# A hybrid SSD and pooling trunk on one core: input transposes and the dt projection moved ahead of the input norm, with the stored transpose as residual

## The chip, the cores and the metric

The kernel runs on one core of a Trainium2 chip. The metric is the device time of one execution in microseconds (us). Engines: PE (tensor engine, with PEld as its weight load), DVE (vector), ACT (scalar), POOL (GpSimd) and SP (which issues DMAs).

## The reference, cut to what matters

272 tokens (16 learned meta tokens and 256 of the input) of width 2048 pass two layers; every sub-layer is wrapped in norms, `h = h + post_norm(f(pre_norm(h)))`. Layer 0 is a Mamba-2 mixer and an FFN, layer 1 a pooling mixer and an FFN. All is float32.

```python
def rmsnorm(x, w):
    return x * rsqrt(mean(x * x, axis=-1) + 1e-6) * w
...
def ssd_mixer(u, w_in, ...):
    z, xBC, dt_raw = split(u @ w_in, [4096, 4096 + 6144])   # the last 64 columns are dt_raw
    xBC = silu(causal_depthwise_conv(xBC, conv_w, conv_b))
    dt = softplus(dt_raw + dt_bias)
    ...
def reference(...):
    h = concatenate([meta, x], axis=1)
    for i in range(2):
        u = rmsnorm(h, norm_w[i, 0])
        mix = ssd_mixer(u, ...) if i % 2 == 0 else pool_mixer(u, ...)
        h = h + rmsnorm(mix, norm_w[i, 1])
        f = swiglu(rmsnorm(h, norm_w[i, 2]), ...)
        h = h + rmsnorm(f, norm_w[i, 3])
    return h[:, 16:]
```

## The kernel before, in words

Activations lie transposed: channels on the 128 partitions, the 272 tokens along the row, as 16 slices of 128 channels. Every weight matrix is cut into panels (`Panel`) of 512 columns as a rule. A panel is streamed in steps: SP loads 512 KB or 1 MB of raw weights into one of three buffers (`emit_dma`, L147), ACT rounds a piece to the format that PE multiplies in one pass (`whi`, `emit_hi`, L162), DVE computes what the rounding left over (`wlo`, `emit_lo`, L175; called the weight rest below), and PE makes three products per 128x128 block: rounded weight with rounded activation, rounded weight with the activation's rest, weight rest with rounded activation (L275 to L277). The activations are kept in the same two parts, `uhi` and `ulo`, the two halves of the tile `uu`. Products of two unrounded fp32 tiles are issued too; the profile shows each of these as two records.

`run_stream` (L241) walks over all steps in a fixed order and emits the casts two steps ahead. Each engine works off its queue in the order in which instructions were emitted. Smaller work is emitted between products as generators (`gen_...`) in three lists, at places set by a rough clock in the program (`Clock`).

`startup` (L1208) loads meta tokens (`mt`) and input (`xt`) with tokens on partitions, sums squares on ACT and DVE into `ssq`, which POOL zeroes first, and makes the factors `rs`. Then, slice by slice and interleaved with the steps of the first panel B0, it scales the tokens (L1283 to L1290), transposes them on PE with three instructions a slice (L1301, L1303), and turns the result into `uhi` (ACT, L1304) and `ulo` (DVE, L1305), both read from PSUM. Panel dt (64 columns, each loaded twice so that all 128 partitions of the result are filled) follows B0 with the usual three products, then come C0 and the panels of x and z. SP issues the eleven small parameter loads (L1233) after the input and the first weights.

For the residual, `gen_h` (L754) loads x and the meta tokens again during panel oB, the output projection's second half, and transposes 8 of the 16 slices between products of oB; the other 8 are transposed in `junction` (L883), at the start of the first FFN, after the row of the norm is finished. The other junctions have seven unused products there (`warm`, L643) that keep PE at work while DVE takes the reciprocal. After it `Producer` makes the normed slices: the sum h, `uu` rounded by ACT (L717), its rest by DVE (L727).

Of the kernel before, what the change touches and what calls it, by code (L numbers as in the profile page):

```python
# [15 lines left out]
P = 128  # L16
# [51 lines left out]
def trunk_kernel(ctx: ExitStack, tc: tile.TileContext, x, meta, norm_w, w_in, conv_w, conv_b,  # L68
# [230 lines left out]
    cs_dram = dram.tile([64, T], F32, name="cs_dram")  # L299
    S = {"conv": 0}  # L300
# [23 lines left out]
    def evac_dt(m, a):  # L324
        S["dtw"] = [S["pool"].tile([P, CBW], F32, name="M", bufs=5) for i in range(5)]
        nc.scalar.activation(out=S["dtw"][0][:, :T], in_=a[:, :T], func=AF.Identity, bias=dtb)

    def gen_dt():
        dtcs = S["dtcs"]
        v, e, z, z2, q = [t[:, :T] for t in S["dtw"]]  # L330
# [3 lines left out]
        t = ck.act(T * 3, f="exp")  # L334
# [418 lines left out]

    def gen_h():  # L754
        f = F["pool"]
        h = F["h"]
        for c in range(4):
            cs_ = slice(c * 512, (c + 1) * 512)
            xr = f.tile([P, 2, 512], F32, name="xr", bufs=2)
            mr = f.tile([NM, 512], F32, name="mr", bufs=2)  # L760
            nc.sync.dma_start(out=xr, in_=x_f[:, cs_].rearrange("(i p) c -> p i c", p=P))
            nc.sync.dma_start(out=mr, in_=meta[:, cs_])
            t = ck.t["PE"] + 4.0
            if c >= 2:
                F["late_h"].append((c, xr, mr))
                yield "PE", t
                continue
            for k in range(4):
                ks_ = slice(k * P, (k + 1) * P)
                yield "py", t  # L770
                tp = bank("py")
                locks.add("py")
                nc.tensor.transpose(tp[:, 0:NM], mr[:, ks_], ident[0:NM, 0:NM])
                for i in range(2):
                    nc.tensor.transpose(tp[:, NM + i * P:NM + (i + 1) * P], xr[:, i, ks_], ident)
                t = ck.pe(0.25)
                yield "ACT", t
                nc.scalar.copy(out=h[:, c * 4 + k, :], in_=tp[:, :T])
                locks.discard("py")
                t = ck.act(T)  # L780
# [137 lines left out]
    p_dt()  # L918
# [289 lines left out]
    def startup(st):  # L1208
        start = st.enter_context(tc.tile_pool(name="start", bufs=1, reuse_waits="tile"))
        xt = start.tile([P, 2, D], F32, name="xt")  # L1210
        mt = start.tile([NM, D], F32, name="mt")
        prow = start.tile([P, 4, P], F32, name="prow")
        nc.scalar.preload_act_table(AF.Sqrt)
        nc.sync.dma_start(out=mt, in_=meta)
        for c in range(2):
            cs_ = slice(c * 1024, (c + 1) * 1024)
            for i in range(2):
                nc.sync.dma_start(out=xt[:, i, cs_], in_=x_f[i * P:(i + 1) * P, cs_])
        nc.sync.dma_start(out=prow[:, 0, :], in_=norm_w.rearrange("a b (k p) -> (a b k) p", p=P))
        emit_dma(2)  # L1220
        cw = conv_w[0].rearrange("a (k p) -> (a k) p", p=P)
        dbc = start.tile([P, 64], F32, name="dbc")
        for dst, src in ((prow[:, 1, :], cw[0:128, :]), (prow[0:64, 2, :], cw[128:192, :]),
# [9 lines left out]
            nc.sync.dma_start(out=dst, in_=src)  # L1233
# [17 lines left out]
        sqd = start.tile([P, 1024], F32, name="sqd")

        def sq_act(i, q, c0, c1):
            n, src = (NM, mt[:, c0:c1]) if i == 2 else (P, xt[:, i, c0:c1])
            nc.scalar.activation(out=sqj[0:n, c0:c1], in_=src, func=AF.Square, accum_out=ssq[0:n, i, q:q + 1])

        def sq_dve(i, q, c0, c1):
            nc.vector.scalar_tensor_tensor(out=sqd[:, 0:c1 - c0], in0=xt[:, i, c0:c1], scalar=1.0,
                                           in1=xt[:, i, c0:c1], op0=ALU.mult, op1=ALU.mult,
                                           accum_out=ssq[:, i, q:q + 1])  # L1260

        sq_act(2, 0, 0, 1024)
        sq_act(2, 1, 1024, 2048)
        sq_act(0, 0, 0, 1024)
        sq_dve(1, 0, 0, 1024)
        sq_act(0, 1, 1024, 2048)
        sq_dve(1, 1, 1024, 1536)
        sq_act(1, 2, 1536, 2048)
        tp = bank("pt")
        nc.tensor.transpose(tp[:, 0:P], prow[:, 0, :], ident)  # L1270
        nc.vector.tensor_copy(out=pv[:, 0:P], in_=tp[:, 0:P])
        nc.vector.tensor_reduce(out=rs, in_=ssq, op=ALU.add, axis=mybir.AxisListType.X)
        nc.scalar.activation(out=rs, in_=rs, func=AF.Sqrt, scale=1.0 / D, bias=eps)
        nc.vector.reciprocal(out=rs, in_=rs)

        ends = (256, 512, 1024, 1536, 2048)
        scaled = [0]

        def scale(k):
            while scaled[0] <= k * P:  # L1280
                c0 = scaled[0]
                c1 = scaled[0] = next(e for e in ends if e > c0)
                nc.scalar.activation(out=mt[:, c0:c1], in_=mt[:, c0:c1], func=AF.Copy, scale=rs[0:NM, 2:3])  # L1283
                nc.vector.tensor_scalar(out=xt[:, 0, c0:c1], in0=xt[:, 0, c0:c1], scalar1=rs[:, 0:1], scalar2=None,
                                        op0=ALU.mult)
                if c0 == 0:
# [64 lines left out]
```

## Time and profile before

| | |
|---|---|
| median of 3 runs | 2398.69 us (2398.11 to 2400.9) |
| profiled execution: own time, span | 2399.69 us, 2397.6 us |
| busy: PE, DVE, ACT, POOL | 99%, 60%, 49%, 1% |
| chain that ended last | PE 96%, DVE 2%, ACT 1% |
| mean granted PE clock | 0.998 of full speed |
| DMA | 418 MB, 174 GB/s |

A row of the timeline gives start, duration, engine, source line, operation, the written tile, the read tiles and the shape; in brackets how long the engine sat idle before and what it waited for. Matmuls are pipelined, so the distance between two starts, and not the duration, is what one costs PE.

### The profile page before, as it was taken

How to read it: one execution, taken by the hardware profiler on the slowest of the kernel's cores; microseconds unless marked ns; L12 is line 12 of the kernel's file. 1: busy time of each engine (PE TensorE's matmuls, PEld its weight loads, DVE VectorE, ACT ScalarE, POOL GpSimd, SP SyncE). 2: the span in 40 equal slices, each digit the busy share in tenths (PEclk: the TensorE clock that was granted, in tenths of full speed). 3: DMA queues.
4: the chain of work that ended last, by engine and by line, in shares of the span. 5: the costliest groups of instructions: out<-in, count | busy, mean ns of one | idle time of the engine just before them, and what ended most of it. 6: DMA issues, size and time to landing. Idle time of an engine off the chain costs nothing.

```text
span 2397.6 us, 39491 instructions
## 1 busy us (share of the span) xinstructions
PE 2364.3 (99%) x16660; PEld 2219.0 (93%) x16660; DVE 1447.8 (60%) x1927; ACT 1180.2 (49%) x1605; POOL 13.8 (1%) x38
## 2 busy tenths in 40 slices
PE   7999999999999999999999999999999999999998
PEld 7999999999999999999999999988888888888886
DVE  5878867647865855454445454578666554556655
ACT  6656565445654644443344443456544444444443
POOL 0000000000000000000000000010000000000000
PEclk9999999999999999999999999999999999999999
DMA  6555555555554555565555555433665655565554
GB/s 190 170 165 182 177 167 176 170 176 178 176 178 158 147 189 175 163 189 176 176 176 173 179 176 176 167 120 106 191 195 173 192 195 192 177 199 187 197 189 141
DMA packets 203825, 418.37 MB, mean 174 GB/s; under 512 B 9920, under 2 KB 10416, under 8 KB 203504
## 3 DMA queue, kind: packets, MB, share of 16 engines
q1 hardware_dynamic: 203216, 415.07, 53.9%
q8 instruction: 130, 2.13, 0.4%
q10 hardware_dynamic: 432, 0.79, 0.1%
q14 instruction: 47, 0.39, 0.0%
HBM read 413.66 MB, written 2.17 MB: 173 GB/s over the span
## 4 chain that ended last, share of the span: by engine, by line
PE 96%; DVE 2%; ACT 1%; issue 0%; DMA 0%; SPq 0%; DVEq 0%; ACTq 0%
PE acc_g L271 7%; PE acc_u L271 7%; PE acc_g L276 4%; PE acc_g L277 4%; PE acc_d L277 4%; PE acc_g L275 4%; PE acc_u L275 4%; PE acc_u L277 4%; PE acc_u L276 4%; PE acc_d L276 4%; PE acc_d L275 4%; PE acc_g L273 3%; PE acc_u L273 3%; PE acc_z L275 3%; PE acc_z L277 3%; PE acc_z L276 3%
## 5 line engine op out<-in xcount | busy, mean ns | idle before, releaser
L175 DVE TENSOR_TENSOR wlo<-raw,whi 128x1024 fp32r<-128x1024 f32 (+2 forms) x804 | 936.9, 1167 | 772.3 <-ACT whi L162 767.7
L162 ACT CAST whi<-raw 128x1024 fp32r<-128x1024 f32 (+2 forms) x800 | 803.1, 1005 | 951.6 <-PE acc_u L276 149.3
L271 PE MATMUL acc_g<-uu,whi 128*128 128x512 f32 x704 | 248.5, 396 | 2.5 <-DVE uu L727 1.3
L271 PE MATMUL acc_u<-uu,whi 128*128 128x512 f32 x704 | 247.0, 394 | 0.2 <-DVE g L789 0.2
L275 PE MATMUL acc_g<-uu,whi 128*128 128x272 f32 x704 | 204.8, 291 | 0.9 <-ACT uu L717 0.9
L277 PE MATMUL acc_g<-uu,wlo 128*128 128x272 f32 x704 | 203.8, 289 | 0.0
L276 PE MATMUL acc_g<-uu,whi 128*128 128x272 f32 x704 | 203.5, 289 | 0.1
L277 PE MATMUL acc_u<-uu,wlo 128*128 128x272 f32 x704 | 203.2, 289 | 0.0
L277 PE MATMUL acc_d<-hidhi,wlo 128*128 128x272 f32 x704 | 203.2, 289 | 0.0
L275 PE MATMUL acc_u<-uu,whi 128*128 128x272 f32 x704 | 203.1, 288 | 0.0
L276 PE MATMUL acc_u<-uu,whi 128*128 128x272 f32 x704 | 202.7, 288 | 0.0
L275 PE MATMUL acc_d<-hidhi,whi 128*128 128x272 f32 x704 | 202.3, 287 | 0.0
L276 PE MATMUL acc_d<-hidlo,whi 128*128 128x272 f32 x704 | 202.2, 287 | 0.0
L273 PE MATMUL acc_g<-uu,wlo 128*128 128x256 f32 x704 | 197.2, 280 | 0.7 <-DVE wlo L175 0.7
L273 PE MATMUL acc_u<-uu,wlo 128*128 128x256 f32 x704 | 197.0, 280 | 0.0
L271 PEld LDWEIGHTS acc_g<-uu,whi 128*128 128x128 f32 x704 | 132.1, 188 | 34.9 <-DVE ups L815 1.9
L271 PEld LDWEIGHTS acc_u<-uu,whi 128*128 128x128 f32 x704 | 132.1, 188 | 32.0 <-DVE g L789 0.6
L275 PE MATMUL acc_z<-uu,whi 128*128 128x272 f32 x512 | 150.7, 294 | 0.0
L275 PE MATMUL acc_x<-uu,whi 128*128 128x272 f32 x512 | 150.2, 293 | 0.0
L277 PE MATMUL acc_x<-uu,wlo 128*128 128x272 f32 x512 | 147.6, 288 | 0.0
L277 PE MATMUL acc_z<-uu,wlo 128*128 128x272 f32 x512 | 147.6, 288 | 0.0
L276 PE MATMUL acc_x<-uu,whi 128*128 128x272 f32 x512 | 147.4, 288 | 0.0
(384 smaller groups left out, 5250.0 us busy)
## 6 DMA issues: line engine op xcount, KB each, us to landing
raw<-in_ffn_w_down_dram SPq DMA_DIRECT2D x88, 1024.0 KB, 5.0
raw<-in_ssd_w_in_dram SPq DMA_DIRECT2D x76, 1024.0 KB, 5.3
raw<-in_ffn_w_gate_dram SPq DMA_DIRECT2D x64, 1024.0 KB, 5.2
raw<-in_ffn_w_up_dram SPq DMA_DIRECT2D x64, 1024.0 KB, 5.2
raw<-in_ssd_w_out_dram SPq DMA_DIRECT2D x32, 1024.0 KB, 5.1
raw<-in_ffn_w_gate_dram SPq DMA_DIRECT2D x32, 768.0 KB, 4.5
raw<-in_ffn_w_up_dram SPq DMA_DIRECT2D x32, 768.0 KB, 4.5
bc<-cs_dram SPq DMA_DIRECT2D x32, 272.0 KB, 6.0
```

Source lines behind the costliest of these rows:

```text
L162: nc.scalar.copy(out=s["hi"], in_=raw)
L175: nc.vector.tensor_tensor(out=s["lo"][:, :, sl], in0=raw, in1=s["hi"].bitcast(F32)[:, :, sl], op=ALU.subtract)
L271: nc.tensor.matmul(a[:, :2 * p.n].rearrange("p (a c) -> p a c", c=p.n), lhsT=wh, rhs=p.both(k), start=st, stop=False)
L273: nc.tensor.matmul(a[:, p.n:2 * p.n], lhsT=wl, rhs=xh, start=False, stop=en)
L275: nc.tensor.matmul(a[:, :p.n], lhsT=wh, rhs=xh, start=st, stop=False)
L276: nc.tensor.matmul(a[:, :p.n], lhsT=wh, rhs=xl, start=False, stop=False)
L277: nc.tensor.matmul(a[:, :p.n], lhsT=wl, rhs=xh, start=False, stop=en)
```

## The change

1. The residual: the transposed raw tokens are kept. They lie in `part`, are written to a DRAM tensor `xT_dram` by four DMAs from POOL, and are read back into `h` by four DMAs from POOL when the FFN's pool opens. `gen_h` and the transposes in `junction` are gone; the first junction gets the seven warming products of the others.
2. The start: all 16 slices of raw tokens are transposed first. ACT copies each into `part`. The dt projection is made from these raw slices with plain fp32 products, two of 64 columns a slice into the two halves of the accumulator, interleaved with the transposes; its weights `wdt` are multiplied by the norm's weights on DVE, and its result by the token factors `rb` in `gen_dt`. The row `rb` is spread over partitions by PE at slice 10.
3. The normed slices are made from `part`: DVE multiplies by weight and `rb`, ACT rounds, DVE subtracts. Five are emitted beside the transposes, the others ahead of B0's steps. B0 is streamed in steps of two slices instead of one.
4. Loads: the norm weights come first, x comes in eight pieces of both token tiles, the meta tokens on ACT's queue, the dt weights between the x pieces, three B0 loads instead of two. The eleven parameter loads are issued by POOL, ahead of its zeroing of `ssq`.

```diff
+    xT_dram = dram.tile([P, KD, T], F32, name="xT_dram")
...
-    def gen_dt():
+    def gen_dt(a):
...
+        nc.vector.tensor_tensor(out=v, in0=a[:, :T], in1=rb, op=ALU.mult)
+        t = ck.dve(T + 60)
+        yield "ACT", t
+        nc.scalar.activation(out=v, in_=v, func=AF.Identity, bias=dtb)
...
-        add_panel(Panel(nm, wi[:, c0:c0 + 512], 16, xhl, T, evac_raw, ku=2 if nm == "B0" else 4, ks=1 if nm == "B0" else 2, 
-                        after=lambda: add_work("A", nm, gen_bc(kind, half))))
+        add_panel(Panel(nm, wi[:, c0:c0 + 512], 16, xhl, T, evac_raw, after=lambda: add_work("A", nm, gen_bc(kind, half))))
...
-        F["late_h"] = []
+        for c in range(4):
+            nc.gpsimd.dma_start(out=F["h"][:, c * 4:c * 4 + 4, :], in_=xT_dram[:, c * 4:c * 4 + 4, :])
...
         def pre():
             if l1 == 0:
-                flush("h")
                 open_hidden()
             F["ss"].row(rb)
-            if l1 == 0:
-                for c, xr, mr in F["late_h"]:
...
-                        nc.scalar.copy(out=F["h"][:, c * 4 + k, :], in_=tp[:, :T])
-            else:
-                F["ss"].warm(WARM)
+            F["ss"].warm(WARM)
             recip(rb, n)
...
     p_bc("B", 0)
-    p_dt()
     p_bc("C", 0)
...
+        nc.scalar.dma_start(out=mt, in_=meta)
+        for c in range(8):
+            cs_ = slice(c * 256, (c + 1) * 256)
+            nc.sync.dma_start(out=xt[:, :, cs_], in_=x_f[:, cs_].rearrange("(i p) c -> p i c", p=P))
+            if c % 4 == 0:
+                k8 = slice(c * 2, c * 2 + 8)
+                nc.sync.dma_start(out=wdt[:, k8, :], in_=wi[c * 256:c * 256 + 1024, 10240:10304].rearrange(
+                    "(k p) c -> p k c", p=P))
+        emit_dma(3)
...
-            nc.sync.dma_start(out=dst, in_=src)
+            nc.gpsimd.dma_start(out=dst, in_=src)
...
         nc.gpsimd.memset(ssq, 0.0)
...
+        def factor_row():
+            tp = bank("py")
+            for n, c0 in parts:
+                nc.tensor.matmul(tp[:, c0:c0 + n], lhsT=ones[0:n, 0:P], rhs=dg[0:n, c0:c0 + n], start=True, stop=True)
+            nc.scalar.copy(out=rb, in_=tp[:, :T])
...
+        def turn(k):
+            ks_ = slice(k * P, (k + 1) * P)
+            tp = acc_tile() if k % 2 else bank("pt")
+            nc.tensor.transpose(tp[:, 0:NM], mt[:, ks_], ident[0:NM, 0:NM])
+            for i in range(2):
+                nc.tensor.transpose(tp[:, NM + i * P:NM + (i + 1) * P], xt[:, i, ks_], ident)
+            nc.scalar.copy(out=part[:, k, :], in_=tp[:, :T])
+
+        def dt_mm(k):
+            for d in range(2):
+                nc.tensor.matmul(acc_dt[64 * d:64 * d + 64, :T], lhsT=wdt[:, k, :], rhs=part[:, k, :],
+                                 start=k == 0, stop=k == KD - 1)
...
+                v = start.tile([P, T], F32, name="v", bufs=3)
+                nc.vector.scalar_tensor_tensor(out=v, in0=part[:, k, :], scalar=nw(0, 0, k), in1=rb, op0=ALU.mult,
+                                               op1=ALU.mult)
+                nc.scalar.copy(out=uhi[:, k, :], in_=v)
+                nc.vector.tensor_tensor(out=ulo[:, k, :], in0=v, in1=uhi[:, k, :].bitcast(F32), op=ALU.subtract)
...
+        nc.scalar.activation(out=sqm[0:NM], in_=mt, func=AF.Square, accum_out=ssq[0:NM, 2, 0:1])
+        dummies(5)
...
+        for k in range(KD):
+            turn(k)
+            if k == 0:
+                dummies(2, P)
...
+                    nc.vector.tensor_tensor(out=wdt[:, k8, :], in0=wdt[:, k8, :], in1=nwk[:, k8, :], op=ALU.mult)
+                    squares(2 * h)
+                    squares(2 * h + 1)
+                factors()
+            else:
+                dt_mm(k - 1)
+            if k == 10:
+                factor_row()
+            if k >= 11:
+                upto(k - 10)
+            if k == 12:
+                emit_hi(1)
+                emit_lo(1)
+        dt_mm(KD - 1)
+        for c in range(4):
+            nc.gpsimd.dma_start(out=xT_dram[:, c * 4:c * 4 + 4, :], in_=part[:, c * 4:c * 4 + 4, :])
 
         def prestep(k0, ks, hook):
-            upto(k0 + ks + 2)
-            if k0 + ks >= KD:
+            upto(k0 + ks + 4)
+            if k0 == 6:
                 params()
+            if k0 == 10:
                 open_ssd()
-
-        upto(1)
+                add_work("A", "dt", gen_dt(acc_dt))
```

Three places in the order of the instructions. Line numbers of the changed kernel are its own.

POOL at the start (its masks, then `ssq`), before:

```order
L96 MEMSET tri 128x432
L98 AFFINE_SELECT tri<-tri 128x272
L98 AFFINE_SELECT tri<-tri 128x144
L98 AFFINE_SELECT tri<-tri 128x16
L1250 MEMSET ssq 128x12
L311 MEMSET dtcs 128x128
```

and of the change:

```order
L98 AFFINE_SELECT tri<-tri 128x16
L1193 DMA prow<-in_ssd_conv_w_dram 128x128
L1193 DMA prow<-in_ssd_conv_w_dram 64x128
L1193 DMA prow<-in_ssd_conv_b_dram 48x128
L1193 DMA prow<-in_ssd_norm_w_dram 32x128
L1193 DMA prow<-in_pool_b_dram 16x128
L1193 DMA prow<-in_pool_scale_dram 16x128
L1193 DMA dbc<-in_ssd_d_dram 128x64
L1193 DMA dtb<-in_ssd_dt_bias_dram 64x1 x2
L1193 DMA acol<-in_ssd_a_log_dram 64x1 x2
L1212 MEMSET ssq 128x12
L1298 DMA xT_dram<-part 128x1088 x4
```

The zeroing of `ssq` now stands behind eleven DMAs.

ACT at the start (`sqm` are the meta tokens' squares, `rs` the square root of the factors, `part` the transposed raw slices), of the change:

```order
L1171 ACT_TABLE_LOAD
L1173 DMA mt<-in_meta_tokens_dram 16x2048
L1271 ACTIVATE sqm,ssq<-mt 16x2048
L1251 COPY part<-pt 128x272
L1225 ACTIVATE rs<-rs,eps 128x3
L1251 COPY part<-acc_start 128x272
L1251 COPY part<-pt 128x272
```

The square root stands between the copies of the first and the second transposed slice; before, all squares and the root came ahead of the first transpose.

DVE during B0 (`v` the normed slice, `uu` its rest, `wlo` the weight rests), before:

```order
L1305 SCALAR_TENSOR_TENSOR uu<-acc_start,pv,uu 128x272
L175 TENSOR_TENSOR wlo<-raw,whi 128x512
L1305 SCALAR_TENSOR_TENSOR uu<-pt,pv,uu 128x272
L175 TENSOR_TENSOR wlo<-raw,whi 128x512
L1284 TENSOR_SCALAR xt<-xt,rs 128x512
```

and of the change:

```order
L175 TENSOR_TENSOR wlo<-raw,whi 128x1024 x2
L1266 SCALAR_TENSOR_TENSOR v<-part,pv,rb 128x272
L1269 TENSOR_TENSOR uu<-v,uu 128x272
L1266 SCALAR_TENSOR_TENSOR v<-part,pv,rb 128x272
L1269 TENSOR_TENSOR uu<-v,uu 128x272
L175 TENSOR_TENSOR wlo<-raw,whi 128x1024
```

A slice costs DVE two instructions instead of one, and ACT's rounding of the slice (`uu<-v`, L1268) lies between the two.

## Rows read from the trace of the kernel before

**Rows 1.** The page's first part: busy time, share of the span, instructions.

```profile
PE 2364.3 (99%) x16660; PEld 2219.0 (93%) x16660; DVE 1447.8 (60%) x1927; ACT 1180.2 (49%) x1605; POOL 13.8 (1%) x38
```

**Rows 2.** Windows: stretch, length, busy of each engine, then clock, DMA share, GB/s.

```profile
49.75:55.78 6.03, 6.03 (x50) 6.03 (x49) 3.41 (x4) 3.29 (x7) 0.00 (x0) 1.00 0.77 261
778.60:782.20 3.60, 3.50 (x14) 3.25 (x15) 3.42 (x9) 2.40 (x6) 0.00 (x0) 0.53 0.02 5
1584.00:1600.00 16.00, 14.88 (x61) 9.60 (x61) 15.62 (x36) 11.34 (x24) 1.59 (x5) 1.00 0.21 65
1610.00:1622.00 12.00, 10.71 (x78) 9.63 (x77) 10.78 (x16) 10.27 (x27) 0.00 (x0) 1.00 0.23 67
```

**Rows 3.** Timeline of PE: B0's first products, dt's last, C0's first.

```profile
15.85 0.58 PE L275 MATMUL acc_B<-uu,whi 128*128 128x272 f32 x1
...
20.45 0.43 PE L276 MATMUL acc_B<-uu,whi 128*128 128x272 f32 x1
20.68 0.43 PE L277 MATMUL acc_B<-uu,wlo 128*128 128x272 f32 x1
...
55.65 0.29 PE L277 MATMUL acc_dt<-uu,wlo 128*128 128x272 f32 x1
55.78 0.29 PE L275 MATMUL acc_C<-uu,whi 128*128 128x272 f32 x1
```

**Rows 4.** Timeline of the first 12 us: POOL, DVE and ACT.

```profile
2.92 0.11 POOL L1250 MEMSET ssq<- 128x12 f32 x1
...
10.32 0.69 DVE L1258 SCALAR_TENSOR_TENSOR sqd<-xt 128x512 f32<-128x512 f32 x1 [1.34 <-DMA xt<-in_x_dram]
...
11.43 0.30 ACT L1273 ACTIVATE rs<-rs,eps 128x3 f32<-128x3 f32 x1 [0.39 <-DVE rs L1272]
```

**Rows 5.** Timeline of SP's queue: the first, the shortest and the last parameter issues.

```profile
5.39 1.21 SPq L1233 DMA_DIRECT2D prow<-in_ssd_conv_w_dram  x2
...
10.25 0.31 SPq L1233 DMA_DIRECT2D prow<-in_pool_b_dram  x1
...
14.40 1.23 SPq L1233 DMA_DIRECT2D acol<-in_ssd_a_log_dram  x2
```

**Rows 6.** Timeline of PE: fp32 products into two column halves, SSD heads.

```profile
141.21 0.29 PE L277 MATMUL acc_z<-uu,wlo 128*128 128x272 f32 x1
141.43 1.00 PE L518 MATMUL py<-M,xd 128*64 128x272 f32 x12
...
141.94 0.41 PE L518 MATMUL py<-M,xd 128*64 128x144 f32 x4
```

**Rows 7.** Groups of instructions by line and form: busy us, mean ns | idle before.

```profile
L175 DVE TENSOR_TENSOR wlo<-raw,whi 128x1024 fp32r<-128x1024 f32 x656 | 801.7, 1223 | 682.8 <-ACT whi L162 682.7
L162 ACT CAST whi<-raw 128x1024 fp32r<-128x1024 f32 x656 | 687.1, 1049 | 833.6 <-PE acc_d L276 142.0 <-PE acc_u L276 111.9 <-PE acc_g L276 97.3
L162 ACT CAST whi<-raw 128x512 fp32r<-128x512 f32 x16 | 9.7, 609 | 0.0
L1305 DVE SCALAR_TENSOR_TENSOR uu<-acc_start,pv,uu 128x272 fp32r<-128x272 f32 x8 | 4.0, 501 | 6.3 <-ACT uu L1304 6.3
```

**Rows 8.** Timeline of the junction (PE, ACT, DVE) and of the pool layer's.

```profile
773.39 0.23 PE L896 MATMUL acc_h<-ident,mr 16*128 16x16 f32 x1
773.92 0.23 PE L896 MATMUL acc_h<-ident,mr 16*128 16x16 f32 x1
...
774.03 4.10 ACT L899 COPY h<-acc_h 128x272 f32<-128x272 f32 x8
...
776.52 0.44 DVE L716 TENSOR_TENSOR h<-h,tmp 128x272 f32<-128x272 f32 x1
778.02 0.52 ACT L717 ACTIVATE uu<-h,pv 128x272 fp32r<-128x272 f32 x1
...
1580.83 3.37 PE L647 MATMUL py<-ones,ident 128*128 128x272 f32 x14
1585.06 0.49 PE L1004 MATMUL acc_tok<-whi,uu 128*128 128x512 f32 x1 [0.85 <-ACT uu L717]
```

More of the change, by code (lines that the diff above doesn't have):

```diff
@@ L333, in gen_dt @@
         nc.scalar.activation(out=v, in_=v, func=AF.Relu)
[L334 removed]
+        t = ck.act(T * 4, f="exp")
         yield "DVE", t
@@ L752, in open_hidden @@
         F["hidlo"] = f.tile([P, 24, T], F32R, name="hidlo")
[L754 to L780, printed above, removed]
     def evac_gate(nt, n, two):
@@ L1245, in params @@
             nc.vector.tensor_scalar(out=acol, in0=acol, scalar1=-1.0, scalar2=None, op0=ALU.mult)
-        sqj = start.tile([P, D], F32, name="sqj")
+        sqd = start.tile([P, 512], F32, name="sqd")
+        sqm = start.tile([P, D], F32, name="sqm")
         ssq = start.tile([P, 3, 4], F32, name="ssq")
         rs = start.tile([P, 3], F32, name="rs")
+        dg = start.tile([P, T], F32, name="dg")
         nc.gpsimd.memset(ssq, 0.0)
[L1251 to L1286, printed above, removed]
-                    nc.vector.tensor_scalar(out=xt[:, 1, c0:c1], in0=xt[:, 1, c0:c1], scalar1=rs[:, 1:2],
-                                            scalar2=None, op0=ALU.mult)
-                else:
-                    nc.scalar.activation(out=xt[:, 1, c0:c1], in_=xt[:, 1, c0:c1], func=AF.Copy, scale=rs[:, 1:2])
@@ new lines, in squares, with factors @@
+        def squares(q):
+            c = slice(q * 512, (q + 1) * 512)
+            for i in range(2):
+                nc.vector.scalar_tensor_tensor(out=sqd, in0=xt[:, i, c], scalar=1.0, in1=xt[:, i, c], op0=ALU.mult,
+                                               op1=ALU.mult, accum_out=ssq[:, i, q:q + 1])
+        parts = ((P, NM), (P, NM + P), (NM, 0))
+        def factors():
+            nc.vector.tensor_reduce(out=rs, in_=ssq, op=ALU.add, axis=mybir.AxisListType.X)
+            nc.scalar.activation(out=rs, in_=rs, func=AF.Sqrt, scale=1.0 / D, bias=eps)
+            nc.vector.reciprocal(out=rs, in_=rs)
+            for i, (n, c0) in enumerate(parts):
+                nc.vector.tensor_scalar(out=dg[0:n, c0:c0 + n], in0=ident[0:n, 0:n], scalar1=rs[0:n, i:i + 1],
+                                        scalar2=None, op0=ALU.mult)
@@ new lines, in factor_row, with dummies @@
+        def factor_row():
[3 more added lines that the diff above has]
+            nc.scalar.copy(out=rb, in_=tp[:, :T])
+        w = bank("py")
+        def dummies(n, cols=T):
+            for _ in range(n):
+                nc.tensor.matmul(w[:, 0:cols], lhsT=ident, rhs=ones[:, 0:cols], start=True, stop=True)
+        acc_dt = acc_tile("dt")
+        def turn(k):
+            ks_ = slice(k * P, (k + 1) * P)
+            tp = acc_tile() if k % 2 else bank("pt")
+            nc.tensor.transpose(tp[:, 0:NM], mt[:, ks_], ident[0:NM, 0:NM])
+            for i in range(2):
+                nc.tensor.transpose(tp[:, NM + i * P:NM + (i + 1) * P], xt[:, i, ks_], ident)
+            nc.scalar.copy(out=part[:, k, :], in_=tp[:, :T])
@@ L1297, in upto @@
                 made[0] += 1
-                scale(0 if k == 0 else min(k + 2, KD - 1))
-                ks_ = slice(k * P, (k + 1) * P)
-                tp = acc_tile() if k % 2 else bank("pt")
-                nc.tensor.transpose(tp[:, 0:NM], mt[:, ks_], ident[0:NM, 0:NM])
-                for i in range(2):
-                    nc.tensor.transpose(tp[:, NM + i * P:NM + (i + 1) * P], xt[:, i, ks_], ident)
-                nc.scalar.activation(out=uhi[:, k, :], in_=tp[:, :T], func=AF.Copy, scale=nw(0, 0, k))
@@ new lines, in upto @@
+                nc.scalar.copy(out=uhi[:, k, :], in_=v)
+                nc.vector.tensor_tensor(out=ulo[:, k, :], in0=v, in1=uhi[:, k, :].bitcast(F32), op=ALU.subtract)
+        nc.scalar.activation(out=sqm[0:NM], in_=mt, func=AF.Square, accum_out=ssq[0:NM, 2, 0:1])
+        dummies(5)
+        tp = bank("pt")
+        nc.tensor.transpose(tp[:, 0:P], prow[:, 0, :], ident)
+        nc.vector.tensor_copy(out=pv[:, 0:P], in_=tp[:, 0:P])
+        for k in range(KD):
+            turn(k)
+            if k == 0:
+                dummies(2, P)
+                nwk = pv[:, 0:KD].unsqueeze(2).to_broadcast([P, KD, 64])
+                for h in range(2):
+                    k8 = slice(h * 8, h * 8 + 8)
+                    nc.vector.tensor_tensor(out=wdt[:, k8, :], in0=wdt[:, k8, :], in1=nwk[:, k8, :], op=ALU.mult)
[11 more added lines that the diff above has]
+                emit_lo(1)
```

27 lines of the change are left out of this document (3 added, 24 removed).

## The prediction

> **What bounds the kernel now.** Read the page's first part first: the tensor engine (PE) is busy for 99% of the span [rows 1]. A change can then gain in two ways only: fewer or cheaper PE instructions, or a shorter stretch in which PE stands still or runs at half its clock. It loses where PE gets a new wait. So the question is where PE is idle or slow now, and the stages at which the edits lie answer it.
>
> The first such stage is the start. The first panel that is wholly free of the start-up work, C of group half 0, begins at 55.78 [rows 3]; everything ahead of it (norm, transposes, panel B0, panel dt) is rebuilt by the change, so "when does C start" is the number to compare. Inside that stretch products of B0 follow each other 0.23 us apart as late as 20.45, at the end of dt 0.13 [rows 3]: PE begins at 1.2 GHz and rises to 2.4. The panel dt alone fills 6.03 us [rows 2], 0.126 for each of its 48 products.
>
> The second stage is the junction ahead of the first FFN. There PE makes eight token transposes in a row, 0.53 us each, then waits for ACT's slice of 778.02; the granted clock of the 3.6 us from 778.6 on is 0.53 [rows 2, 8].
>
> **The edits, term by term.** All times are of the profiled execution (2399.69 us, span 2397.6), which lies 1.0 us above the median of 2398.69; the forecast is put against the median at the end.
>
> *Late edits, gains.* Sixteen residual transposes go. Eight of them stand between products of panel oB and eight at the junction; one costs 0.53 us of PE from start to start [rows 8]. The eight in oB give 8 x 0.53 = 4.2 us, all of it on the path, since PE has no gap there. At the junction the PE time of the eight is not the limit; the ACT copies behind them are: they run until 778.1, while the sum h is ready at 776.96, so the first `uu` slice comes at 778.02 instead of about 776.97 [rows 8]. That is 1.05 us. The seven warming products that replace them (14 records in 3.37 us [rows 8]) end before the first slice is there and cost nothing. The stretch at 0.53 of the clock holds 3.6 us; at the full clock its work takes half, so 1.7 us more come back if the warming products keep the clock up. Sum of gains: 4.2 + 1.05 + 1.7 = 7.0 us. The four writes of the transposes to DRAM and the four reads back (0.54 MB each) replace reads of the same size; they are issued when the pool opens, with three panels of oB still to come (192 products of 0.126 each, 24 us a panel), so I cost them at nothing. If that cover were gone, h would be late and PE would wait for it.
>
> *When can the chain of the start begin?* In the changed order ACT makes the meta squares, then the copy of transpose 0, then the square root of the factors, and only then the copy of transpose 1. The square root waits for eight DVE squares over all of x; the dt product of k = 1 waits for that copy. So PE stands from about its second dt pair until the square root is done; call that T0. Two things set it.
>
> (a) The landing of x. Now the last half megabyte lands at 10.32, after DVE had waited 1.34 us for it [rows 4]. 0.5 MB of dt weights and the norm vectors are queued ahead of the end of x, about 1.5 us more: 11.8. Then two squares of 0.7, and from the end of the last square (11.0) to that of the square root (11.7) 0.7 as now [rows 4]: T0 = 13.9 at the earliest.
>
> (b) The zeroing of `ssq`. Every square adds into it. Now POOL zeroes it at 2.92 [rows 4]; the change puts the eleven parameter DMAs ahead of it on POOL. The trace has no DMA issued from POOL. From below: the shortest issue on SP is 0.31 us [rows 5], eleven make 3.4, zeroing at 6.4, and (a) would decide. From above: the same eleven took SP from 5.39 to 15.63, with waits for earlier transfers in between [rows 5], 10.2 us, so zeroing at 13.2. POOL's ninth to eleventh also wait for earlier ones to complete, so I take a value near the upper row: 12. Behind it DVE has eight squares of 0.7 (5.6), one scaling of dt weights of 0.6 (as a 512-wide rest) and the 0.7: T0 = 18.9. The Trainium skill ("DMA: Bandwidth & Descriptors", Specifications) gives about 1 us to the first byte for a DMA issued from GpSimd; an estimate of eleven in a row by that figure puts the zeroing at 14 and the time 2 us above mine; no run shown here has such a DMA.
>
> *From T0 to the factor row R.* PE then has nine dt pairs, eight transpose triples and the row of factors. A triple is 0.53 us at the full clock [rows 8]. A pair (two fp32 products into the two column halves) is priced by the same form in the SSD heads: both 272-column products start at 141.43 and the next piece at 141.94, so the halves run together in 0.51; entering costs 0.22 instead of 0.126 [rows 6], so I add 0.1 each way: 0.71. That makes 9 x 0.71 + 8 x 0.53 = 10.6, plus 1.4 for the first copy and for the row with its copy: 12 us at the full clock, 23 at half. PE comes out of a wait, as at the present start, and I take as long a stretch at half clock as there (from 15.85 until just after 20.68 [rows 3]), 5 us, of which half is lost: 14.5. R = 33.4.
>
> *From R to the end of B0.* Here DVE and ACT, not PE, set the pace. Each slice of `uu` is now three steps in a row: DVE multiplies (0.50), ACT rounds (0.40, by line through the 512 and 1024 casts of 0.61 and 1.05), DVE subtracts (0.44, the price of the sum of h) [rows 7, 8], with hand-offs 1.4. DVE can't use the gap, because the subtraction stands ahead of the next multiplication in its queue. A step of B0 needs two slices, and behind them a weight rest of 1.2, which waits another 0.6 for the 1.05 cast that ACT starts after the second slice: 2.8 + 0.6 + 1.2 = 4.6 us against 24 x 0.126 = 3.0 us of PE. Counted on DVE from R: six slices 8.4, rests 0 to 2 with one wait 4.2, five such rounds 23.0, small parameter copies and the first dt operation 1.5, PE's last step 3.0: 40 us. C starts at 33.4 + 40 = 73.4. It started at 55.78. The loss is 17.6 us, with the 6.03 us of the old dt panel already in it. The extra dt work on DVE after that has the same length as now.
>
> **Sum.** +17.6 - 7.0 = +10.6: 2410.3 on the profiled execution, **2409 us** against the median of 2398.69: slower by 0.4%. About 0.2% (4.8 us) is what a measurement of this kernel can tell from no change, so the same means 2393.9 to 2403.5. Break-even would need R at 55.8 + 7.0 - 40 = 22.8. With T0 at 13.9 and the full clock at once R is 25.9, which is the low end of this case: +3.1, or 2402. The high end, with zeroing at 13.2, is 2411; a whole start at half clock comes under the first rival.
>
> **Rivals.**
> 1. *The clock stays low through the dt stretch.* For it: at the junction a stretch of transposes alone, then about 1 us of waiting, ended at a granted clock of 0.53 [rows 2, 8], and the dt stretch is transposes and short pairs in turn. Against it: in the pool stage PE mixed short work and idle time (10.71 of 12.00 busy) at 1.00 [rows 2]. Then T0 to R is 23 instead of 14.5, and 1 us less of R to C is lost on DVE: +7.5, so 2417; with the upper T0 2418, and 2421 if the first two steps of B0 also run at half clock (6.0 us each in place of 4.6).
> 2. *DVE keeps up and the start is early, so it is not slower.* The mechanism is in B0: if the three-step slices overlapped (a subtraction beside the next multiplication, or the casts ahead of time) so that a round stayed under PE's 3.0 us, B0 would take 8 x 3.0 and a little. With T0 at 13.9 and the full clock, the dt stretch ends near 33, C starts near 58, and the 7 us of gains remain: -5, or 2394. It decides from a round below 3.0 us. Against it: the order of DVE's queue and three prices that each have a row [rows 7]. For it: none of these three has been seen in just this sequence.
> 3. *The late gains don't come.* If the clock falls at the junction as before, or h comes late from DRAM, some or all of 7 us is missing: 2411 to 2416. The junction ahead of the pool layer speaks against it: there the warming products end at 1584.20, the next one starts at 1585.06, and no low clock follows [rows 2, 8].
>
> **How the numbers follow.** Main case 0.58, low clock 0.16, not slower 0.20, late gains missing 0.06. Slower by over 0.2%: nearly all of the main case (0.54), the low clock and the missing gains, 0.76. The not-slower case lies on the border of 0.2% below and is halved: 0.10 faster; the other half and the low edge of the main case make 0.14 the same. The range leaves out most of the not-slower case and nothing else: 2399 to 2421. The main case alone spans 2402 to 2413.
>
> **What would show it.** In the profile after: POOL's zeroing of `ssq` at 10 to 14 and the first DVE square behind it; ACT's square root at about 19; transposes and dt pairs until about 41; the row of factors near 33; DVE waits on ACT of about 0.45 per slice; weight rests on DVE 4.6 us apart in B0, PE waiting for them 1.6 us a step; C at about 74. Late: oB without transposes, the first FFN product at about 777.5 plus the shift, at full clock. It would be wrong if `ssq` were zeroed early and C began before 63, or if the rounds of B0 came out at 3 us.

## The result, and the profile after

The changed kernel took 2415.2 us (median of 6 runs, 2413.4 to 2416.5), the kernel before 2398.8 beside it: ratio 1.0066, 95% interval 1.0053 to 1.0079. It is slower by 0.7%. The forecast was 2409 with a range of 2399 to 2421, slower: the sign holds and the time lies in the range, 6 us above the number. The profiled execution of the change, the shortest of the six, took 2413.36 us; its span is 2411.7, 14.1 more than before, where the sum said 10.6. (The medians are 16.4 apart.)

Part 1 of the page after answers to [rows 1]. PE is busy for 11 us more, with two instructions more:

```profile
PE 2375.4 (98%) x16662; PEld 2219.5 (92%) x16662; DVE 1453.5 (60%) x1943; ACT 1165.8 (48%) x1575; POOL 23.9 (1%) x57
```

Three first products cut the span into stages. The timeline of PE before has the second of them, oB's first product, and the third, the FFN's:

```profile
668.15 0.29 PE L275 MATMUL acc_oB<-yhi,whi 128*128 128x272 f32 x1
...
778.60 0.43 PE L275 MATMUL acc_g<-uu,whi 128*128 128x272 f32 x1 [0.90 <-ACT uu L717]
```

The same view after, with C's first product, two waits of PE inside C, and the pool layer's first product:

```profile
74.00 0.29 PE L275 MATMUL acc_C<-uu,whi 128*128 128x272 f32 x1
...
80.66 0.39 PE L277 MATMUL acc_C<-uu,wlo 128*128 128x272 f32 x1 [0.21 <-DVE wlo L175]
...
85.89 0.55 PE L363 MATMUL pt<-ident,M 128*128 128x128 f32 x3 [0.70 <-DVE M L356]
...
687.76 0.29 PE L275 MATMUL acc_oB<-yhi,whi 128*128 128x272 f32 x1
...
788.67 3.37 PE L643 MATMUL py<-ones,ident 128*128 128x272 f32 x14
792.92 0.39 PE L275 MATMUL acc_g<-uu,whi 128*128 128x272 f32 x1 [0.88 <-ACT uu L713]
...
1598.28 0.50 PE L960 MATMUL acc_tok<-whi,uu 128*128 128x512 f32 x1 [0.84 <-ACT uu L713]
```

With 55.78 and 1585.06 from [rows 3, 8] the difference splits without a rest:

| stage | before | after | difference | forecast |
|---|---|---|---|---|
| start to C | 55.78 | 74.00 | +18.2 | +17.6 |
| C to oB | 612.37 | 613.76 | +1.4 | 0 |
| oB to FFN | 110.45 | 105.16 | -5.3 | -5.25 (4.2 + 1.05) |
| FFN to pool layer | 806.46 | 805.36 | -1.1 | -1.7 |
| pool layer to end | 812.54 | 813.42 | +0.9 | 0 |
| sum | 2397.6 | 2411.7 | +14.1 | +10.6 |

The late edits do what was said: no transpose in oB, the warming products over long before the first slice. The start loses about what was said, but by another path. The start's timeline (POOL, DVE, ACT and PE) shows it, beside [rows 4]:

```profile
2.92 1.24 POOL L1193 DMA_DIRECT2D prow<-in_ssd_conv_w_dram  x2
...
9.58 0.52 POOL L1193 DMA_DIRECT2D acol<-in_ssd_a_log_dram  x1 [0.40 <-DMA prow<-in_ssd_conv_b_dram]
10.08 0.13 POOL L1212 MEMSET ssq<- 128x12 f32 x1
10.24 0.69 DVE L1217 SCALAR_TENSOR_TENSOR sqd<-xt 128x512 f32<-128x512 f32 x1 [3.11 <-POOL ssq L1212]
10.24 1.91 ACT L1271 ACTIVATE sqm<-mt 16x2048 f32<-16x2048 f32 x1 [8.15 <-POOL ssq L1212]
...
12.56 1.17 PE L1255 MATMUL acc_dt<-part,wdt 128*64 128x272 f32 x4 [4.72 <-ACT part L1251]
16.87 0.30 ACT L1225 ACTIVATE rs<-rs,eps 128x3 f32<-128x3 f32 x1 [4.36 <-DVE rs L1224]
17.49 1.17 PE L1255 MATMUL acc_dt<-part,wdt 128*64 128x272 f32 x4 [2.92 <-ACT part L1251]
19.42 1.18 PE L1255 MATMUL acc_dt<-part,wdt 128*64 128x272 f32 x4
...
34.70 0.68 PE L1255 MATMUL acc_dt<-part,wdt 128*64 128x272 f32 x4
35.84 0.68 PE L1255 MATMUL acc_dt<-part,wdt 128*64 128x272 f32 x4
```

POOL zeroes `ssq` at 10.08 (forecast 12), DVE and ACT wait for that, and PE stands twice behind ACT's copies, 4.72 and 2.92 us. The second time it is the square root of 16.87 that holds the copy, and it ends at T0 = 17.2 (forecast 18.9). Then the dt pairs come 1.94 us apart (17.49 to 19.42 and on to 31); behind that, at 34.70 and 35.84, they are 1.14 apart. The windows say why (columns as in [rows 2]; the second-last row is the whole of B0):

```profile
17.40:32.10 14.70, 14.61 (x53) 5.63 (x53) 0.61 (x3) 3.02 (x9) 1.12 (x2) 0.50 0.47 181
32.10:42.34 10.24, 8.49 (x54) 4.14 (x52) 5.11 (x10) 5.01 (x12) 0.81 (x2) 1.00 0.14 56
42.47:74.00 31.53, 28.83 (x197) 27.72 (x196) 21.04 (x39) 17.20 (x30) 1.73 (x6) 0.89 0.40 133
792.92:796.52 3.60, 3.45 (x25) 3.25 (x26) 3.42 (x9) 2.39 (x6) 0.00 (x0) 1.00 0.02 5
```

PE has next to no gap from 17.4 to 32.1 and runs at 1.2 GHz all the while. Ahead of that it had stood still twice, and the clock fell within the first of these waits: the granted clock is 0.82 from 10.0 to 12.5 and 0.50 from 12.5 to 17.4. At the junction the clock now is 2.4 GHz, where before it was 0.53 of that [rows 2].

One round of B0 on DVE, between two weight rests (timeline of DVE and ACT):

```profile
50.70 1.23 DVE L175 TENSOR_TENSOR wlo<-raw,whi 128x1024 fp32r<-128x1024 f32 x1 [0.51 <-ACT whi L162]
51.84 0.50 DVE L1266 SCALAR_TENSOR_TENSOR v<-part,pv,rb 128x272 f32<-128x272 f32 x1
52.37 0.42 ACT L1268 CAST uu<-v 128x272 fp32r<-128x272 f32 x1 [1.70 <-DVE v L1266]
52.82 0.44 DVE L1269 TENSOR_TENSOR uu<-v,uu 128x272 fp32r<-128x272 f32 x1 [0.49 <-ACT uu L1268]
53.18 0.50 DVE L1266 SCALAR_TENSOR_TENSOR v<-part,pv,rb 128x272 f32<-128x272 f32 x1
...
54.16 0.44 DVE L1269 TENSOR_TENSOR uu<-v,uu 128x272 fp32r<-128x272 f32 x1 [0.48 <-ACT uu L1268]
55.11 1.23 DVE L175 TENSOR_TENSOR wlo<-raw,whi 128x1024 fp32r<-128x1024 f32 x1 [0.51 <-ACT whi L162]
```

The three waits forecast are there, 0.49, 0.48 and 0.51, and the round is 4.41 us (forecast 4.6) against 3.0 of PE.

### The profile page after: what moved, and what is told of

Its sections match the earlier page's. It is cut to its first block, busy times and chain, and to the rows that moved or that the text cites. A ratio compares the mean times of both kernels' runs of the same rounds, so it can differ in the third digit from the quotient of the medians.

```text
span 2411.7 us, 39497 instructions
## 1 busy us (share of the span) xinstructions
PE 2375.4 (98%) x16662; PEld 2219.5 (92%) x16662; DVE 1453.5 (60%) x1943; ACT 1165.8 (48%) x1575; POOL 23.9 (1%) x57
## 4 chain that ended last, share of the span: by engine, by line
PE 93%; DVE 4%; ACT 2%; issue 1%; DMA 0%; POOL 0%; DVEq 0%; ACTq 0%; POOLq 0%
PE acc_g L271 7%; PE acc_u L271 7%; PE acc_d L277 4%; PE acc_u L275 4%; PE acc_u L277 4%; PE acc_u L276 4%; PE acc_d L276 4%; PE acc_d L275 4%; PE acc_g L277 4%; PE acc_g L275 4%; PE acc_g L276 4%; PE acc_g L273 3%; PE acc_u L273 3%; PE acc_z L275 3%; PE acc_z L277 3%; PE acc_z L276 3%
## 5 line engine op out<-in xcount | busy, mean ns | idle before, releaser
L175 DVE TENSOR_TENSOR wlo<-raw,whi 128x1024 fp32r<-128x1024 f32 (+1 forms) x792 | 933.5, 1181 | 769.4 <-ACT whi L162 765.3
L162 ACT CAST whi<-raw 128x1024 fp32r<-128x1024 f32 (+1 forms) x792 | 801.5, 1013 | 953.7 <-PE acc_u L276 149.3
```

Of the source, the lines that this page charges most:

```text
L162: nc.scalar.copy(out=s["hi"], in_=raw)
L175: nc.vector.tensor_tensor(out=s["lo"][:, :, sl], in0=raw, in1=s["hi"].bitcast(F32)[:, :, sl], op=ALU.subtract)
```

## The experiments

T0 is the end of the square root, R the first `v` on DVE, C0 the first product of C, all of the profiled execution, whose own time stands beside them. The median and the ratio are of all executions, each ratio to the kernel before on the same chip. Executions of one kernel differ (e2 2406.0 to 2414.4, e10 2407.6 to 2415.2, e7 2392.1 to 2402.5), so a C0 belongs with the time of its own execution and not with the median.

| kernel | T0 | R | C0 | its time | median | ratio (95%) |
|---|---|---|---|---|---|---|
| the change | 17.2 | 34.8 | 74.0 | 2413.4 | 2415.2 | 1.0066 (1.0053 to 1.0079) |
| e1 zeroing first | 17.5 | 36.7 | 76.6 | 2415.9 | 2415.9 | 1.0077 (1.0063 to 1.0091) |
| e2 products ahead | 18.1 | 34.2 | 67.3 | 2406.0 | 2410.5 | 1.0049 (1.0036 to 1.0061) |
| e3 root later | 23.1 | 31.9 | 71.1 | 2410.5 | 2410.5 | 1.0051 (1.0038 to 1.0064) |
| e4 waits filled, 20 and 14 | 18.7 | 36.1 | 75.3 | 2421.2 | 2421.6 | 1.0097 (1.0083 to 1.0111) |
| e6 waits filled, 9 and 6 | 17.2 | 28.8 | 68.0 | 2407.3 | 2407.6 | 1.0043 (1.0030 to 1.0056) |
| e5 old residual | 18.6 | 37.0 | 76.2 | 2422.9 | 2422.2 | 1.0093 (1.0076 to 1.0109) |
| e7 e1, e2 and e3 | 16.7 | 22.6 | 55.8 | 2394.3 | 2394.3 | 0.9986 (0.9977 to 0.9995) |
| e8 old start, late edits | 13.0 | | 65.1 | 2403.3 | 2400.8 | 1.0006 (0.9997 to 1.0014) |
| e9 e7, row at slice 8 | 16.4 | 18.8 | 55.5 | 2393.5 | 2394.4 | 0.9984 (0.9975 to 0.9993) |
| e10 e1, dt weights last | 15.3 | 28.9 | 68.2 | 2407.6 | 2412.1 | 1.0053 (1.0040 to 1.0067) |

**e1: does the zeroing set the start?**

```diff
+        nc.gpsimd.memset(ssq, 0.0)
         cw = conv_w[0].rearrange("a (k p) -> (a k) p", p=P)
...
-        nc.gpsimd.memset(ssq, 0.0)
```

> Only POOL's zeroing of ssq stands ahead of the eleven parameter DMAs again. Theory (the zeroing sets the start, and R and C follow it one for one): the zeroing falls from 10.08 to about 3, the meta squares and the copy of slice 0 come first, the eight DVE squares run back to back from about 7.1 (there DVE began to wait), 6.2 us long, so the square root ends at about 14.1 in place of 17.17; the row slice R moves from 34.8 to about 31.7 and C0 from 74.0 to about 70.9; time about 2412.1. Rival (the low clock sets it): the dt stretch begins earlier but the clock rises no earlier than at 32.1, and R moves by less than 1.5 us: 2413.7 or more.

Not alone: the theory falls. With the zeroing at 2.91 DVE's squares wait for x instead (timeline of DVE and ACT):

```profile
15.52 0.69 DVE L1217 SCALAR_TENSOR_TENSOR sqd<-xt 128x512 f32<-128x512 f32 x1 [0.95 <-DMA xt<-in_x_dram]
...
17.25 0.30 ACT L1225 ACTIVATE rs<-rs,eps 128x3 f32<-128x3 f32 x1 [8.73 <-DVE rs L1224]
17.45 0.36 ACT L1251 COPY part<-acc_start 128x272 f32<-128x272 f32 x1
```

The last piece of x comes at 15.4, so T0 stays. The copy of slice 0 is earlier (8.14), that of slice 1 is not, PE's two waits become one of 6.14, and its dt pairs are 1.94 apart to the end of the stretch: R is later by 1.9. (The clock's own records begin late in this run; the distance of the pairs tells it.) The rival had R nearly unmoved behind an earlier dt stretch; that did not come either. Nor can the 1.9 be put down to the edit alone: the warming products that begin at 4.58 in both kernels took 2.02 us here and 1.19 in the change, so here the clock was low already ahead of the wait.

**e10: what holds x?** From e1, the two loads of dt weights go behind the eight of x, their scaling on DVE behind the squares.

```diff
         for c in range(8):
             cs_ = slice(c * 256, (c + 1) * 256)
             nc.sync.dma_start(out=xt[:, :, cs_], in_=x_f[:, cs_].rearrange("(i p) c -> p i c", p=P))
+        for c in range(8):
             if c % 4 == 0:
                 k8 = slice(c * 2, c * 2 + 8)
...
```

> As the kernel with the zeroing first, with the two loads of dt weights (0.5 MB in rows of 256 bytes) issued behind the eight pieces of x, and their scaling on DVE behind the squares. There the last piece of x came at 15.4, where 11.8 was predicted. Theory (the dt weights ahead of x hold it): x lands by 12, squares end at 13.4, the square root at about 14. Rival (the eight pieces of x in rows of 1 KB are slower than the four loads of before in rows of 4 KB, 10.32): the last piece comes at 13.5 or later and the square root at 15 or later. The time follows the square root one for one if the clock rises after the same work: 2412.5 by the theory, 2414 by the rival.

The dt weights held it: DVE's last two squares start at 11.55 and 12.29, back to back, so all of x is there by 11.5, at least 3.9 us earlier (timeline of DVE):

```profile
11.55 0.69 DVE L1218 SCALAR_TENSOR_TENSOR sqd<-xt 128x512 f32<-128x512 f32 x1
...
14.25 0.69 DVE L1286 TENSOR_TENSOR wdt<-wdt,pv 128x512 f32<-128x512 f32 x1 [0.66 <-DMA wdt<-in_ssd_w_in_dram]
```

The square root came at 15.3 all the same, since the reduction now stands behind the scaling. The 0.5 MB in rows of 256 bytes cost 3.9 us, as if at about 130 GB/s, where the forecast gave them 1.5; at the 285 GB/s that all transfers together moved in e1 from 5 to 15.4 they would take 1.8. The Trainium skill ("DMA: Bandwidth & Descriptors", Specifications) asks for at least 512 bytes per transfer for the full rate; this pair of runs agrees.

T0 is 2.2 earlier than in e1, R 7.8. The rest is the clock, which is low here for a shorter time, though PE had waited 4.95 us: 0.50 up to 20.5 (window, columns as in [rows 2]) and 1.00 from there to R.

```profile
13.70:20.50 6.80, 6.76 (x25) 2.62 (x25) 1.56 (x6) 1.73 (x5) 0.59 (x1) 0.50 1.01 384
```

Why it rose behind 6.8 us of work here and behind 14.6 in the change, no run tells.

**e3: the square root behind slice 6.**

```diff
-                factors()
             else:
                 dt_mm(k - 1)
+            if k == 6:
+                factors()
```

> The reduction, the square root and what follows it are issued after the copy of slice 6 in place of after that of slice 0. Theory (the square root in ACT's queue holds the copy of slice 1, and with it PE from 14.6 to 17.5): PE goes on with the second dt pair at about 14.6, R moves by 3 from 34.8 to 31.8, if the clock rises after as much work as before; C0 at 71: about 2412.2. Rival (the clock rises at a fixed place or the pause is what lowers it): with the clock full through the stretch R comes at about 26 and the time is 2406; with the clock rising only at 32.1 as before R moves by 1.5 at most: 2413.7 or more.

R 31.9 and C0 71.1, as the theory said. ACT's copies no longer wait for the root, and the root itself, late as it is, holds nobody (timeline of ACT):

```profile
14.79 0.39 ACT L1251 COPY part<-pt 128x272 f32<-128x272 f32 x1 [1.82 <-PE pt L1250]
...
22.83 0.30 ACT L1225 ACTIVATE rs<-rs,eps 128x3 f32<-128x3 f32 x1
```

The copies now wait for PE, still 1.94 us apart: the low clock remains (granted 0.50 from 12.7 to 29.2).

**e4 and e6: PE's waits filled with warming products**, in front of the first two dt pairs (20 and 14 in e4, 9 and 6 in e6).

```diff
             else:
+                if k < 3:
+                    dummies(9 if k == 1 else 6)
                 dt_mm(k - 1)
```

> 20 warming products are put into PE's first wait (7.8 to 12.5) and 14 into its second (14.5 to 17.5), nothing else changes. Theory (PE's pauses let the clock fall, and at half clock a slice of the dt stretch takes 1.94 us against 1.14): the clock is full from 12.6 on, eight slices save 0.8 each, so R comes at about 28.5 in place of 34.8 and C0 near 67.7: about 2409. Rival (the dt stretch itself, short pairs and transposes, does not hold the clock): it falls again within the stretch, R is at 34 to 37.5, time 2415 to 2418.

> As the kernel with filled waits, with 9 and 6 warming products in place of 20 and 14: one takes 0.48 us of PE at the full clock, so 9 and 6 fit into the waits of 4.7 and 3 us. Theory (PE's two pauses let the clock fall and the low clock costs 0.8 us a slice): full clock from 5 on, dt slices 1.14 apart, R at 29 to 30 in place of 34.8 and C0 near 69: about 2410. Rival (with so few products the clock falls again, or the fillers are as dear as what they save): R at 33 or later, 2414 or more.

In e4 the theory's mechanism came, its time did not: the pairs behind the fillers are 1.14 apart, but 20 fillers lasted 9.33 us in a wait of 4.7, and 14 lasted 6.58 in one of 3. A filler takes 0.47 us of PE; e4 was sized with half of that. e6 has the right number (timeline of PE):

```profile
8.32 4.29 PE L1241 MATMUL py<-ones,ident 128*128 128x272 f32 x18
12.63 0.68 PE L1255 MATMUL acc_dt<-part,wdt 128*64 128x272 f32 x4
...
13.68 2.92 PE L1241 MATMUL py<-ones,ident 128*128 128x272 f32 x12
17.56 0.68 PE L1255 MATMUL acc_dt<-part,wdt 128*64 128x272 f32 x4 [0.96 <-ACT part L1251]
...
18.70 0.68 PE L1255 MATMUL acc_dt<-part,wdt 128*64 128x272 f32 x4
```

The granted clock behind the fillers is 1.00 (window):

```profile
17.55:27.80 10.25, 10.24 (x64) 4.98 (x64) 0.54 (x3) 3.32 (x9) 1.12 (x2) 1.00 0.67 259
```

T0 and the pairs' begin are those of the change (17.2 and 17.6), R is 6.0 earlier, C0 too: the low clock in the dt stretch costs the change 6.0 us, and PE's standing still ahead of it brings it about: the traces of the kernels in which the two waits are filled or gone (e4, e6, e7 and e9) don't have it. That holds for the profiled executions. Three of e6's five took 2407.3 to 2407.6 at a mean granted clock of 0.997 to 0.999, the other two 2413.5 and 2413.9 at 0.994; whether the low clock came back in these, no trace shows.

**e2: the products v one step ahead.** Each step of B0 makes the two products of the next step before the two subtractions of its own.

```diff
+            mul(k1)
+            for k in ks_:
+                nc.scalar.copy(out=uhi[:, k, :], in_=vs[k])
+            mul(k1 + ahead)
+            for k in ks_:
...
-            upto(k0 + ks + 4)
+            upto(k0 + ks + 4, 2)
```

> In B0 the DVE products v are made one step ahead (both products of the next step stand before the two subtractions of this one), everything else is the same. Theory (the three operations in a row and the wait for the cast of weights make the round of 4.41): DVE has 2 x (0.50 + 0.44) + 1.22 = 3.1 per round and no wait left, so weight rests come 3.1 to 3.3 us apart, C0 begins at about 68 in place of 74.0: about 2409.5. Rival (ACT, or a shared port, sets the round): the rests stay at least 4 us apart and the time is 2413 or more.

The timeline of DVE in B0, from one weight rest to the next:

```profile
48.32 1.22 DVE L175 TENSOR_TENSOR wlo<-raw,whi 128x1024 fp32r<-128x1024 f32 x1
49.46 0.91 DVE L1266 SCALAR_TENSOR_TENSOR v<-part,pv,rb 128x272 f32<-128x272 f32 x2
50.28 0.79 DVE L1280 TENSOR_TENSOR uu<-v,uu 128x272 fp32r<-128x272 f32 x2
50.99 1.22 DVE L175 TENSOR_TENSOR wlo<-raw,whi 128x1024 fp32r<-128x1024 f32 x1
```

No wait is left, and a round takes 2.67 in place of 4.41, less even than the 3.1 expected, because two operations of a kind in a row take 0.91 and 0.79, not twice 0.50 and 0.44. From R to C0 it takes 33.2 in place of 39.2: the three-step slice in the order of DVE's queue costs 6 us. ACT is not the limit. Nor is the clock: over B0 it is 0.89 in the change, 1.00 here, but in e10, with the change's order, it is 1.00 too, and R to C0 takes the same 39.2.

**e5: the start alone.** The residual is made from transposes again.

```diff
-        for c in range(4):
-            nc.gpsimd.dma_start(out=F["h"][:, c * 4:c * 4 + 4, :], in_=xT_dram[:, c * 4:c * 4 + 4, :])
+        F["late_h"] = []
...
                 open_ffn()
+                add_work("B", "h", gen_h())
```

> The changed start alone: the residual comes again from 16 token transposes (eight among the products of oB, eight at the junction) and is neither written to DRAM nor read back. Theory (the late edits are worth what the two traces show between the first oB product and the first product of the FFN, 110.44 against 105.16, and behind it, 18.46 against 17.36 for the first stretch of gate products): 6.4 us slower than the change, 2421.6. Rival (these stretches differ for another reason, such as the place of the clock's fall): 2417 or less.

2422.2, 7.0 above the change (e5's own start was 2.2 later). The timeline of PE has oB's first product and the FFN's:

```profile
690.03 0.29 PE L275 MATMUL acc_oB<-yhi,whi 128*128 128x272 f32 x1
...
800.47 0.59 PE L275 MATMUL acc_g<-uu,whi 128*128 128x272 f32 x1 [0.90 <-ACT uu L712]
```

Between them lie 110.44 us again. In the change and in the nine other kernels with the late edits it is 105.15 to 105.17. From the FFN's first product to the pool layer's e5 takes 2.3 more than the change; the granted clock at its junction is 0.50 from 800.1 to 806.9.

**e8: the late edits on the old start.** The residual is here the transposed normed token times the square root.

```diff
+                nc.scalar.copy(out=part[:, k, :], in_=tp[:, :T])
...
+                        nc.gpsimd.tensor_tensor(out=part[:, k, :], in0=part[:, k, :], in1=rb2, op=ALU.mult)
```

> The kernel before with the late edits alone: its start also copies each transposed slice of normed tokens, POOL multiplies the copies by a row of the square roots, so that they are the raw tokens again, and writes them to DRAM; the transposes in oB and at the junction go. Theory (the late gain of 6.4 does not hang on the new start; 16 ACT copies of 0.4 hide beside the rounds of B0 of 4.07 PE): one row of factors more on PE, under 1 us, so 2392.5 to 2393.5. Rival (ACT, with 0.8 us more per round, sets the round of B0): C0 later by up to 6, 2398 or more.

The rival's time came, and worse: C0 at 65.1, 9.3 later. In ACT's queue the new copy waits for DVE's rest of the slice, and the cast of weights stands behind it (timeline of ACT):

```profile
39.44 0.39 ACT L1282 COPY part<-pt 128x272 f32<-128x272 f32 x1 [0.93 <-DVE uu L1279]
39.73 0.62 ACT L162 CAST whi<-raw 128x512 fp32r<-128x512 f32 x1
...
41.68 0.39 ACT L1282 COPY part<-acc_start 128x272 f32<-128x272 f32 x1 [0.94 <-DVE uu L1279]
```

That makes 2.23 us per slice, where PE's work is 2.04. ACT stands idle 0.93 of them, so here it is not its busy time but the order that costs. Sixteen times 0.19 is 3.0 of the 9.3; the rest lies ahead of these slices (T0 is 1.3 later, PE waits 1.78 and 1.62 ahead of B0) and was not taken apart. The late edits gain here too (105.15 from oB to the FFN), and the start eats it up: 2400.8, no difference to before.

**e7: e1, e2 and e3 together**, and **e9**: the row of factors after slice 8 in place of 10.

> The zeroing first, the square root behind slice 6 and the products of DVE one step ahead, together. Theory (PE's start has no pause left: the first copy comes at about 8.1, dt pairs follow at 1.14 per slice at the full clock, slice 10 and the square root at 17.5 are there at about 20): R at 21 to 23, B0 paced by DVE and PE at 2.7 to 3.0 per round, C0 at 54 to 57, time 2395 to 2398. Rival (the clock is low through the dt stretch without pauses too): 1.94 per slice, R at 28 to 30, C0 at 61 to 63, time 2402 to 2405.

> As the three edits together, with the row of factors made after slice 8 in place of slice 10, and the slices of normed input begun two turns sooner. Theory (with the three edits PE is the bound again up to C: its last dt product is at 30 and 192 products of 0.126 follow, so C0 can't come before 54.4): R at about 20.3 in place of 22.6, C0 at 54.4 to 55.2 in place of 55.8, so 2393 to 2394, no difference that can be told. Rival (R still sets C0): C0 earlier by about 2, time 2392 or less.

Timeline of PE in e7:

```profile
9.71 1.18 PE L1255 MATMUL acc_dt<-part,wdt 128*64 128x272 f32 x4
11.41 0.68 PE L1255 MATMUL acc_dt<-part,wdt 128*64 128x272 f32 x4
12.55 0.68 PE L1255 MATMUL acc_dt<-part,wdt 128*64 128x272 f32 x4
...
55.80 0.29 PE L275 MATMUL acc_C<-uu,whi 128*128 128x272 f32 x1
```

The pairs are 1.14 apart from 11.4 on, without a filler; C begins at 55.80, the kernel before had 55.78. So the rebuilt start costs nothing any more and the late gains show: the median is 2394.3, below that of before by 0.14% (0.05 to 0.23), which is less than the 0.2% that the prediction calls the least that can be told, and below the change by 21 us. The parts don't add (e1 alone gave nothing, e3 and e2 3 and 7 us at C0; together 18): with the pauses gone the clock holds as well. In e9 R is 3.8 earlier and C0 0.3: PE is the bound again, as the theory said.

## Why the forecast was right, and where not

- **Sign and main mechanism: right.** The start loses 18.2 (17.6 forecast), and B0's rounds behind a three-step slice are a large part: e2 gives 6 us back by reordering DVE alone. That also settles the second rival: a DVE round below 3.0 exists (2.67), but not in the order of this change. Its start is reachable too (e7), with three edits that the change doesn't have.
- **T0: the bounds held, the reason was half of it.** 17.2 lay inside 13.9 to 20.1. In path (b) the zeroing was put too late: the first eight issues on POOL begin 0.62 us apart or less, then come three waits of 0.4 to 0.5, so eleven end at 10.08, not at 12. The Trainium skill ("DMA: Bandwidth & Descriptors", Specifications) has about 1 us to the first byte of such a DMA; taken as the time of an issue it gave 14, and this trace does not bear that out. The step that failed is path (a): "about 1.5 us more" for the dt weights ahead of x, for which the prediction gave no row, hence 13.9. It is 17.5 (e1), because they cost 3.9 (e10, by moving them). Both paths end within 0.4 us of each other, so undoing either alone gains little.
- **T0 to R: mis-sized, 14.5 against 17.6.** Its full-clock value, 12, is good: 11.5 in e6. The failed step is "as long a stretch at half clock as there", 5 us: it lasted from before 17.4 until 32.1. So the first rival, given 0.16, came in its mechanism for most of the stretch; its price of 23 was too high, since a slice takes 1.94 at 1.2 GHz, not twice 1.14: e1, low from T0 to R, needs 19.2. "PE comes out of a wait" was the right reason: e6's profiled execution and e7's, where the waits are filled or gone, have no such stretch. How long it lasts did not follow from the wait: behind its last wait PE ran at 1.2 GHz for 14.6 us in the change, 10.8 in e2, 16.5 in e5 and 6.8 in e10, which is near the forecast's 5.
- **R to C0: 39.2 against 40**, slice 1.34 against 1.4, round 4.41 against 4.6.
- **Late gains: 5.3 + 1.1 = 6.4 against 7.0.** 4.2 + 1.05 is 5.25: measured 5.3, and 5.3 once more in e5. The clock stays up at the junction, but that gives back 1.1, not 1.7; why 0.6 less was not tried. That h comes from DRAM costs nothing, as said.
- **What was costed at nothing and wasn't: the dt work on DVE in C, +1.4.** It "has the same length as now", but in C it now stands ahead of a weight rest, and PE waits for it at 80.66 and 85.89, 0.9 us together. It was not tried separately; in e2 and e7, where DVE reaches it earlier, C takes 24.4 in place of 25.8 (24.1 before; 0.3 of it comes back by oB).
- The last 0.9 lies behind the pool layer's first product. PE's work there is as long as before (767.17 from the first `acc_mix` product to the last of all, in both traces); 0.2 is a wait ahead of it, and 0.7 lies behind PE's last product, to the end of the span (9.77 before, 10.46 after). Why was not tried.

So the sum of 10.6 was near 14.1 partly because errors cancelled: T0 1.7 too late against 3.1 too little for the clock, and the terms missing in C and at the end make most of the rest.

## What to carry over

Before a start is rebuilt around an engine that runs without gaps, write down each in-order queue (ACT's, DVE's) instruction by instruction: here three orders, a root ahead of a copy, a subtraction ahead of the next product and a zeroing behind DMA issues, made 18 us of loss with the low clock that came of them, and no operation had to go to win them back. Price PE's work behind a pause at the low clock until a trace shows otherwise (how long it stays low is not to be had from the wait), and fill a pause only by as much as it lasts. Where two paths end together, one experiment that shortens one of them and finds nothing does not acquit it.

## What was not expected of the hardware

- 0.5 MB in rows of 256 bytes delayed 2 MB of x behind it by 3.9 us (e1 and e10).
- Half the clock does not double a slice of transposes and fp32 pairs: 1.94 against 1.14.
- Two DVE products in a row take 0.91, one alone 0.50 (e2).
- The clock can fall far from any edit. In e4 the pool layer's stretch below, with the same code as in the other kernels, ran at 1.2 GHz without a gap on PE, and from `acc_mix` to the end it took 784.2 us against 777.7 in the change; that makes most of e4's 2421.6. Why there, no run here tells. The window in e4:

```profile
1637.20:1650.70 13.50, 13.50 (x56) 12.96 (x56) 8.73 (x19) 4.97 (x12) 0.00 (x0) 0.50 0.01 1
```
